# S5 outputs of a channel block as one group of eight matmuls, phase tables in a shared buffer

## The chip, the cores and the metric

The kernel runs on one core of a Trainium2 chip. The metric is the device time of one execution in microseconds; three executions of the kernel before took 1635.12, 1636.76 and 1636.93 us, so the median is 1636.76 us. A separate execution was recorded by the hardware profiler, and all traces and durations below are from that one.

## What is computed

One layer of a hybrid encoder on 256 tokens of width 2048, in float32. After a norm, `w_in` projects every token to 12288 columns. These feed three mixers (a gated linear recurrence called RG-LRU, a chunked attention, an S5 state space), and a sigmoid gate for each. The gated mixers are summed and projected by `w_out`; a SwiGLU feed-forward layer and a last norm follow. The change is in the S5 branch, which in the reference is

```python
bu_re = jnp.einsum("bsgh,gph->bsgp", ug, bb_re)      # 16 channels of group g -> 64 states
bu_im = jnp.einsum("bsgh,gph->bsgp", ug, bb_im)
_, _, xs_re, xs_im = lax.associative_scan(_complex_lin_op, (ar, ai, bu_re, bu_im), axis=1)
y = (jnp.einsum("bsgp,ghp->bsgh", xs_re, c_re) - jnp.einsum("bsgp,ghp->bsgh", xs_im, c_im))
y = y.reshape(b_, s_, SSM_W) + d * uf                # 1024 channels: 64 groups of 16
```

## The kernel before

**The main stream.** All large products run on TensorE as one long list of steps. A step loads 512 KB of weights (256 rows by 512 columns, the tile `raw`, three buffers, issued on the SP queue, L170), splits them into two parts of lower precision whose sum is exact (ScalarE casts `hi` at L123, VectorE subtracts to get `lo` at L124, seven buffers each), and multiplies them with the tokens: for both halves of the tokens and each of two weight tiles three matmuls, L198, L199 and L200, into the PSUM tiles `mm`. So a step has twelve matmuls of 512 columns, and PE has no pause between steps as long as `hi` and `lo` are there in time.

**Background work.** The three mixers are Python generators (`gen_lru`, `gen_att`, `gen_s5`). After each step `bg_mix` runs a few pieces of them, up to a budget; each `yield` states what the piece cost, and a negative number ends the generator's turn. This sets the order in which the program is written. A scheduler then orders the instructions of each engine: it may move an instruction ahead of ones written earlier where its operands and buffers allow it, and the weight loads and splits have a raised priority. Each engine then works through its own list, and semaphores hold an instruction until its operands are there.

**S5.** `gen_s5` treats the 1024 channels as eight blocks of 128 (`b`). A block has four state tiles of 128 states, `jj` 0 to 3, worked through in two halves of two tiles each (`sb`). For a block PE transposes the small B and C matrices and the input (L669 to L671), ScalarE copies `ct` (the C matrices, 32 channels for each state tile) and `uf` (the input) out of PSUM, `bu` and `bc` become operands for the input products. For each half:

- the phase tables: ScalarE scales a ramp (`q`, L702), VectorE reduces it (L703, L704; `w` is a second buffer), ScalarE takes the absolute value (L705), a sine (L706, `tab1`) and a cosine (L707, `tab0`);
- PE makes the input products `bu_re` and `bu_im` (L711, L712), and VectorE rotates them (L720 to L726), scans (L729, L730) and rotates back (L732 to L738), in `m1` and `m2` (tile `sA`) and `m3` and `m4` (tile `sB`). `m1` ends as the real part of the states (L734), `m2` as the imaginary part (L738);
- the output, `out_part`: for each of the two state tiles two matmuls (L745 for the real part, L746 for the imaginary) with a stationary operand of 128 x 32, so each uses one of four groups of 32 array columns and writes 32 PSUM partitions of `y_ps`. L748 adds the input times `d` for the 64 channels of the half and writes the result back to `u`.

The output of the first half is kept in a list (`pend`) until the tables of the second half have been written, that of the second half follows at the end of the block. `sA` has one buffer for `bu` and both halves, and so has `sB`; `q` and `w` have buffers of their own, `sq` and `sw`. All PSUM tiles of the mixers share four buffers (`sm`).

`drain("s5")` writes whatever is left of S5 when the main stream comes to the products that need its output, behind 224 steps; the GELU at L759 and two splits follow.

## Time and profile before

| | us |
|---|---|
| median of three executions | 1636.76 |
| the profiled execution, from its first to its last instruction | 1637.8 |
| PE busy with matmuls in it | 1612.1 |
| DVE busy | 1111.4 |
| ACT busy | 951.6 |
| matmuls L745 and L746, busy | 18.0 and 15.6 |
| first and last of them, start | 116.2 and 705.2 |

PE, DVE and ACT are TensorE, VectorE and ScalarE, and PEld is TensorE's loading of the stationary operand. A row of the timeline has the start in us from the span's first instruction, the length, the engine, the line, what is written and read, and how many instructions the row merges. The recorded end of a matmul is modelled and overlaps the next one; what one costs is read from the starts. A float32 matmul of this kind is two records, so the 64 matmuls in the program are 128 records in the trace.

### The profile page before, as it was taken

The page shows a single profiled execution, that of the slowest core. Times are in us where ns is not written, and L with a number is a line of the kernel's source. Part 1 is how long each engine was busy: PE and PEld are TensorE (multiplying, and loading weights), DVE is VectorE, ACT ScalarE, POOL GpSimd, SP SyncE. Part 2 cuts the span into 40 slices and gives each one's busy share as a digit, 9 for nine tenths or more (in the row PEclk, how much of TensorE's full clock was granted, in tenths as well). Part 3 has the DMA queues.
Part 4 walks back from the last instruction along what each step waited for, and adds up shares of the span by engine and source line. Part 5 has one row for each costly group of instructions (what it writes and reads, how often), then busy time and mean ns, then how long its engine had stood idle before and what let it go on. Part 6 is the DMA issues. An engine that isn't in the chain of part 4 may idle for free.

```text
span 1637.8 us, 21032 instructions
## 1 busy us (share of the span) xinstructions
PE 1612.1 (98%) x7263; PEld 1307.1 (80%) x7263; DVE 1111.4 (68%) x1910; ACT 951.6 (58%) x1696; POOL 0.8 (0%) x6
## 2 busy tenths in 40 slices
PE   7999999999999999999999999999999999999997
PEld 4877877778888777778888888888888888888886
DVE  4869889879697978876666555555555555555654
ACT  4677677675768676665455554555444455455443
POOL 0000000000000000000000000000000000000000
PEclk9999999999999999999999999999999999999999
DMA  8665566655554646565666666666666666666564
GB/s 224 198 178 150 166 183 185 186 165 174 165 177 146 197 152 214 170 201 185 214 236 182 193 191 190 185 192 190 187 192 196 193 187 194 190 192 186 188 191 144
DMA packets 169933, 304.21 MB, mean 186 GB/s; under 512 B 22185, under 2 KB 26721, under 8 KB 169057
## 3 DMA queue, kind: packets, MB, share of 16 engines
q1 hardware_dynamic: 153104, 292.66, 59.5%
q10 hardware_dynamic: 16720, 10.20, 2.3%
q8 instruction: 57, 0.93, 0.2%
q14 instruction: 52, 0.42, 0.1%
HBM read 300.71 MB, written 2.11 MB: 185 GB/s over the span
## 4 chain that ended last, share of the span: by engine, by line
PE 86%; DVE 5%; ACT 3%; DMA 3%; issue 2%; ACTq 0%; DVEq 0%
PE mm L199 27%; PE mm L200 27%; PE mm L198 27%; DMA raw<-in_w_in 3%; DVE lo L124 2%; ACT hi L123 1%; PE y_ps L746 1%; PE mm L957 1%; PE at_ps L241 1%; PE mm L956 1%; PE mm L958 1%; PE y_ps L745 0%; ACT bc L691 0%; DVE xc L470 0%; ACT bc L692 0%
## 5 line engine op out<-in xcount | busy, mean ns | idle before, releaser
L124 DVE TENSOR_TENSOR lo<-raw,hi 128x512 fp32r<-128x512 f32 x1088 | 736.9, 688 | 441.6 <-ACT hi L123 438.9
L123 ACT CAST hi<-raw 128x512 fp32r<-128x512 f32 x1088 | 658.7, 621 | 611.9 <-DVE lo L124 322.2
L199 PE MATMUL mm<-lo,xth 128*128 128x512 f32 x768 | 304.8, 397 | 2.6 <-DVE lo L124 2.6
L200 PE MATMUL mm<-hi,xtl 128*128 128x512 f32 x768 | 302.7, 394 | 0.0
L198 PE MATMUL mm<-hi,xth 128*128 128x512 f32 x768 | 284.2, 396 | 9.6 <-ACT hi L123 9.6
L200 PE MATMUL mm<-hi,h2l 128*128 128x512 f32 x704 | 275.0, 391 | 0.0
L198 PE MATMUL mm<-hi,h2h 128*128 128x512 f32 x704 | 274.9, 390 | 0.0
L199 PE MATMUL mm<-lo,h2h 128*128 128x512 f32 x704 | 274.0, 389 | 0.0
L198 PEld LDWEIGHTS mm<-hi,xth 128*128 128x128 f32 x768 | 144.0, 189 | 46.5 <-ACT hi L123 13.7
L199 PEld LDWEIGHTS mm<-lo,xth 128*128 128x128 f32 x768 | 145.0, 189 | 39.5 <-DVE lo L124 8.3
L200 PEld LDWEIGHTS mm<-hi,xtl 128*128 128x128 f32 x768 | 145.2, 189 | 29.4 <-issue 0.4
L199 PEld LDWEIGHTS mm<-lo,h2h 128*128 128x128 f32 x704 | 132.2, 188 | 27.3
L200 PEld LDWEIGHTS mm<-hi,h2l 128*128 128x128 f32 x704 | 132.1, 188 | 27.2
L198 PEld LDWEIGHTS mm<-hi,h2h 128*128 128x128 f32 x704 | 132.2, 188 | 26.8
L198 PE MATMUL mm<-hi,at 128*128 128x512 f32 x312 | 121.6, 390 | 0.0
L200 PE MATMUL mm<-hi,at 128*128 128x512 f32 x312 | 121.6, 390 | 0.0
L199 PE MATMUL mm<-lo,at 128*128 128x512 f32 x312 | 121.4, 389 | 0.0
L199 PEld LDWEIGHTS mm<-lo,at 128*128 128x128 f32 x312 | 58.6, 188 | 12.2
L200 PEld LDWEIGHTS mm<-hi,at 128*128 128x128 f32 x312 | 58.6, 188 | 12.2
L198 PEld LDWEIGHTS mm<-hi,at 128*128 128x128 f32 x312 | 58.6, 188 | 11.9
L200 PE MATMUL mm<-hi,mtl 128*128 128x512 f32 x128 | 50.3, 393 | 0.0
L199 PE MATMUL mm<-lo,yc 128*128 128x512 f32 x128 | 50.1, 391 | 0.0
(312 smaller groups left out, 1624.7 us busy)
## 6 DMA issues: line engine op xcount, KB each, us to landing
raw<-in_w_in SPq DMA_DIRECT2D x190, 512.0 KB, 4.2
raw<-in_w_ffn_gate SPq DMA_DIRECT2D x88, 512.0 KB, 4.0
raw<-in_w_ffn_up SPq DMA_DIRECT2D x88, 512.0 KB, 3.7
raw<-in_w_ffn_down SPq DMA_DIRECT2D x88, 512.0 KB, 4.7
raw<-in_w_branch SPq DMA_DIRECT2D x48, 512.0 KB, 4.1
raw<-in_w_out SPq DMA_DIRECT2D x32, 512.0 KB, 4.6
raw<-in_ssm_w_glu SPq DMA_DIRECT2D x16, 512.0 KB, 4.7
xa<-in_x SPq DMA_DIRECT2D x8, 256.0 KB, 3.8
```

The costliest lines, as they stand in the source:

```text
L123: act.copy(dst_hi, src)
L124: vec.tensor_sub(dst_lo, src, dst_hi.bitcast(F32))
L198: pe.matmul(acc[h], xh[:, k, hs], hi, start=k == 0, stop=False)
L199: pe.matmul(acc[h], xh[:, k, hs], lo, start=False, stop=False)
L200: pe.matmul(acc[h], xl[:, k, hs], hi, start=False, stop=k == kt - 1)
L241: pe.transpose(t[:, i * S + h * P:i * S + (h + 1) * P], src(h, kt0 + i), ident)
L746: pe.matmul(yp[rs, :S], ct[:, 1, rs], m2[:, i, :], start=False, stop=True)
L956: pe.matmul(last_acc[h], ah[:, k, hs], hi, start=k == 0, stop=False)
L957: pe.matmul(last_acc[h], ah[:, k, hs], lo, start=False, stop=False)
L958: pe.matmul(last_acc[h], al[:, k, hs], hi, start=False, stop=k == kt - 1)
```

## The change

```diff
-            bu = mx.tile([P, 2, 2, S], F32R, tag="sA", name="bu")
+            bu = mx.tile([P, 2, 2, S], F32R, tag="sA", name="bu", bufs=2)
...
+            ys = []
             for sb in range(2):
                 j0 = 4 * b + 2 * sb
-                q = mx.tile([P, 2, S], F32, tag="sq", name="sq")
-                w = mx.tile([P, 2, S], F32, tag="sw", name="sw")
+                qw = mx.tile([P, 2, 2, S], F32, tag="sB", name="qw")
+                q, w = qw[:, 0], qw[:, 1]
...
-                if pend:
-                    pend.pop()()
-                    yield 0.3
-                ma, mb = (mx.tile([P, 2, 2, S], F32, tag=t, name=t) for t in ("sA", "sB"))
+                ma = mx.tile([P, 2, 2, S], F32, tag="sA", name="sA", bufs=2)
+                mb = mx.tile([P, 2, 2, S], F32, tag="sB", name="sB")
...
-                def out_part(b=b, sb=sb, m1=m1, m2=m2, ct=ct, uf=uf, yb=yb):
-                    yp = sm("y_ps")
-                    for i in range(2):
-                        jj = 2 * sb + i
-                        rs = slice(32 * jj, 32 * jj + 32)
-                        pe.matmul(yp[rs, :S], ct[:, 0, rs], m1[:, i, :], start=True, stop=False)
-                        pe.matmul(yp[rs, :S], ct[:, 1, rs], m2[:, i, :], start=False, stop=True)
-                    rr = slice(64 * sb, 64 * sb + 64)
-                    vec.scalar_tensor_tensor(yb[rr], uf[rr], prm[rr, R_D + b:R_D + b + 1], yp[rr, :S],
-                                             ALU.mult, ALU.add)
-                pend.append(out_part)
+                ys.append((m1, m2))
                 yield 1.8
-                if sb == 1:
-                    yield -0.1
-                    pend.pop()()
-                    yield 0.3
+            yield -0.1
+            yp = sm("y_ps")
+            for part in range(2):
+                for jj in range(4):
+                    rs = slice(32 * jj, 32 * jj + 32)
+                    pe.matmul(yp[rs, :S], ct[:, part, rs], ys[jj // 2][part][:, jj % 2, :],
+                              start=part == 0, stop=part == 1)
+            vec.scalar_tensor_tensor(yb, uf, prm[:, R_D + b:R_D + b + 1], yp[:, :S], ALU.mult, ALU.add)
+            yield 0.3
```

The eight output matmuls of a block are now written together: the real parts of all four state tiles, then the imaginary parts. One `y_ps` takes all 128 channels, and one VectorE instruction (L748) finishes them. `sA` has a second buffer, so that the states of both halves live until then. `q` and `w` become two halves of a tile `qw` that takes turns with `m3` and `m4` in the one buffer `sB`. Line numbers shift a little: the tables stay at L702 to L707, the eight matmuls are all at L746, L748 is still the last step, and the rotations and scans between are two lower (the last addition of a half is L736 and was L738, the first products with the tables are L718 to L721 and were L720 to L723).

The list of PE around the output of the second block, first half, before:

```order
L198 MATMUL mm<-hi,xth 128x512
L746 MATMUL y_ps<-sA,ct 32x256
L745 MATMUL y_ps<-sA,ct 32x256
L746 MATMUL y_ps<-sA,ct 32x256
L199 MATMUL mm<-lo,xth 128x512
L200 MATMUL mm<-hi,xtl 128x512
```

and the middle of the second block's output now:

```order
L198 MATMUL mm<-hi,ya_1276 128x512
L199 MATMUL mm<-lo,ya_1276 128x512
L200 MATMUL mm<-hi,ya_1277 128x512
L746 MATMUL y_ps<-sA,ct 32x256 x4
L198 MATMUL mm<-hi,ya_1276 128x512
L199 MATMUL mm<-lo,ya_1276 128x512
```

The scheduler did not leave the matmuls where they were written. Before, a half's output stood in one piece of four matmuls (3 times of 16) or as a single real-part matmul and, some rows later, the other three (13 times): 29 visits of PE to this kind of work. Now it is one piece of eight (blocks 0 and 3) or, for the other six blocks, three pieces: the two real parts of the first half as soon as these are there, four matmuls (the real parts of the second half and the imaginary parts of the first, which use four different column groups), and the last two. That makes 20 visits.

The list of ACT around the tables of the second half of block 1, before (the tables made here are `tab_2458` and `tab_2457`; the `sq` and `sw` written behind them are already those of the next phase):

```order
L706 ACT_TABLE_LOAD
L706 ACTIVATE tab_2458<-sq 128x512
L702 ACTIVATE sq<-cst,s5par 128x256 x2
L123 CAST hi<-raw 128x512 x2
L346 ACT_TABLE_LOAD
L346 ACTIVATE merged<-merged 128x512
L707 ACT_TABLE_LOAD
L707 ACTIVATE tab_2457<-sw,cst 128x512
L123 CAST hi<-raw 128x512 x4
L705 ACTIVATE sw<-sq 128x512
```

and now, where all five belong to the same tables:

```order
L702 ACTIVATE qw<-cst,s5par 128x256 x2
L123 CAST hi<-raw 128x512
L519 DMA rbs<-in_attn_rel_bias 8x257
L123 CAST hi<-raw 128x512 x2
L705 ACTIVATE qw<-qw 128x512
L706 ACT_TABLE_LOAD
L706 ACTIVATE tab_2430<-qw 128x512
L123 CAST hi<-raw 128x512
L707 ACTIVATE tab_2429<-qw,cst 128x512
```

The ramp, the reduction and the absolute value no longer run a phase ahead, since their buffer is free only when the half before is done. The whole list of ACT has 35 loads of function tables, and had 32.

The list of DVE at the same place now, from the last addition of the first half (L736) to the first products of the second (L720, L718):

```order
L736 TENSOR_TENSOR sA<-sA,sB 128x512
L124 TENSOR_TENSOR lo<-raw,hi 128x512 x2
L663 TENSOR_TENSOR bx<-s5bb,cst 128x128 x2
L703 TENSOR_SCALAR qw<-qw 128x512
L124 TENSOR_TENSOR lo<-raw,hi 128x512
L704 SCALAR_TENSOR_TENSOR qw<-qw 128x512
L124 TENSOR_TENSOR lo<-raw,hi 128x512
L520 COPY rbs<-rbs 8x127
L124 TENSOR_TENSOR lo<-raw,hi 128x512
L720 TENSOR_TENSOR sA<-tab_2430,bu_im 128x512
L124 TENSOR_TENSOR lo<-raw,hi 128x512
L718 TENSOR_TENSOR sA<-tab_2429,bu_re 128x512
```

Before, L703 and L704 between two halves belonged to the tables of the next phase, and those of this one were already made. Between L704 and L718 stand three `lo` splits here, and two or three in the other blocks. In five of the eight blocks (this one among them) ACT also loads a function table ahead of L706 between the two halves.

More of the change, by code (lines that the diff above doesn't have):

```diff
@@ L650, in gen_s5 @@
         yield 1.8
-        pend = []
         for b in range(8):
```

## The prediction

> **What bounds the kernel now.** I read the page first: the busy time of each engine and the chain of work that ended last.
>
> ```profile
> span 1637.8 us, 21032 instructions
> PE 1612.1 (98%) x7263; PEld 1307.1 (80%) x7263; DVE 1111.4 (68%) x1910; ACT 951.6 (58%) x1696; POOL 0.8 (0%) x6
> PE 86%; DVE 5%; ACT 3%; DMA 3%; issue 2%; ACTq 0%; DVEq 0%
> ```
>
> PE is busy nearly all the time and carries 86% of the chain. So whatever PE no longer has to do comes off the end, as long as its operands keep up. S5's outputs run from 116 to 705 us, so I then read the busy times of that stretch beside those of the rest, and the groups and waits of the stretch.
>
> ```profile
> 100.00:707.00 607.00, 601.80 (x2748) 476.64 (x2747) 517.08 (x899) 420.12 (x789) 0.00 (x0) 1.00 0.59 175
> 707.00:1637.00 930.00, 921.68 (x4136) 762.00 (x4135) 531.09 (x812) 468.11 (x782) 0.00 (x0) 1.00 0.63 191
> PE mm L198 <- ACT hi L123: 3.1, 7, 0.9
> PE mm L199 <- DVE lo L124: 1.5, 3, 0.9
> L124 DVE TENSOR_TENSOR lo<-raw,hi 128x512 fp32r<-128x512 f32 x392 | 258.8, 684 | 67.5 <-ACT hi L123 66.3
> ```
>
> The columns of the first two rows are the stretch, its length, then the busy time of PE, PEld, DVE, ACT and POOL, the granted clock, the DMA share and GB/s. In the S5 stretch PE is idle for 607.0 - 601.8 = 5.2 us, of which 4.6 are waits for a `hi` or a `lo`. The clock is full. DVE is the next engine, with 517.1 of 607 us; it has 89.9 us idle, 66.3 of them waiting for a cast. DMA is no limit: without S5 the same kind of stream draws 191 GB/s, in the stretch only 175, and 12 us less would ask for 175 x 607 / 595 = 179.
>
> **What an output visit costs PE now.** The timeline of PE over the first block's first half shows both common shapes.
>
> ```profile
> 114.71 0.39 PE L198 MATMUL mm<-hi,xth 128*128 128x512 f32 x1
> ...
> 115.84 0.39 PE L200 MATMUL mm<-hi,xtl 128*128 128x512 f32 x1
> 116.16 0.62 PE L745 MATMUL y_ps<-sA,ct 128*32 128x256 f32 x2
> 116.71 0.50 PE L198 MATMUL mm<-hi,xth 128*128 128x512 f32 x1
> 117.05 0.39 PE L199 MATMUL mm<-lo,xth 128*128 128x512 f32 x1
> 117.28 0.40 PE L200 MATMUL mm<-hi,xtl 128*128 128x512 f32 x1
> 117.60 0.40 PE L746 MATMUL y_ps<-sA,ct 128*32 128x256 f32 x1
> 117.61 0.40 PE L745 MATMUL y_ps<-sA,ct 128*32 128x256 f32 x1
> 117.84 0.38 PE L746 MATMUL y_ps<-sA,ct 128*32 128x256 f32 x1
> 117.85 0.38 PE L745 MATMUL y_ps<-sA,ct 128*32 128x256 f32 x1
> 118.06 0.59 PE L746 MATMUL y_ps<-sA,ct 128*32 128x256 f32 x2
> 118.59 0.50 PE L198 MATMUL mm<-hi,xth 128*128 128x512 f32 x1
> 118.93 0.40 PE L199 MATMUL mm<-lo,xth 128*128 128x512 f32 x1
> ```
>
> A step of the main stream is (115.84 - 114.71) / 5 = 0.226 us, from start to start. The visit with one output matmul (two records) takes 117.05 - 115.84 = 1.21 us from the `mm` ahead to the second `mm` behind; two steps of the stream are 0.45, so the visit costs 0.76 us. The visit with three takes 118.93 - 117.28 = 1.65, so 1.20. Inside it L746 of one state tile and L745 of the next start 0.01 us apart and run beside each other: they use different groups of 32 array columns. The third matmul needs the group of the second and follows. So three matmuls are two rounds, a round costs 1.20 - 0.76 = 0.44 us, and the visit itself 0.76 - 0.44 = 0.32 us (0.32 us from the `mm` ahead in place of 0.23, and 0.5 in place of 0.39 for the first `mm` behind). The three visits with all four matmuls look like this:
>
> ```profile
> 209.91 0.39 PE L200 MATMUL mm<-hi,xtl 128*128 128x512 f32 x1
> 210.23 0.63 PE L745 MATMUL y_ps<-sA,ct 128*32 128x256 f32 x4
> 210.69 0.61 PE L746 MATMUL y_ps<-sA,ct 128*32 128x256 f32 x4
> 211.23 0.50 PE L198 MATMUL mm<-hi,xth 128*128 128x512 f32 x1
> 211.57 0.40 PE L199 MATMUL mm<-lo,xth 128*128 128x512 f32 x1
> ```
>
> From 209.91 to 211.57 is 1.66, less 0.45 is 1.21: two rounds, the L745 of both tiles beside each other and then both L746. In all, before: 13 visits of one (9.9 us), 13 of three (15.6) and 3 of four (3.6), together 29.1 us; of the shares, 29 x 0.32 = 9.3 us is for entering and leaving and 45 rounds make 19.8.
>
> **The same after.** The matmuls are the same 64 and none is shorter; what changes is how many run beside each other and how often PE goes there. By the instruction list there are 20 visits: 12 with two matmuls of one kind (two column groups, one round), 6 with four matmuls in four different column groups, and 2 with eight (all four groups twice). No row of the trace has more than two groups at once. Bounds: all four run beside each other, at 0.01 us for each further start, so a piece of four is one round and a piece of eight two; or only pairs do, so they are two and four rounds. The nearest row, the pair at 117.60, shows no slowing of either (0.44 us for the round, as for a lone matmul), so I take four at once, and 0.04 for the starts.
>
> - Four at once: 12 x 0.77 + 6 x 0.80 + 2 x 1.24 = 9.2 + 4.8 + 2.5 = 16.5 us. Saved: 29.1 - 16.5 = 12.6 us.
> - Pairs: 9.2 + 6 x 1.22 + 2 x (0.32 + 4 x 0.44) = 9.2 + 7.3 + 4.2 = 20.7 us. Saved: 8.4 us.
>
> The Trainium skill, "TensorE: Matmul & The Clock Gate", section on the measured speedup of packing small matmuls, has three column tiles at 2.38 times a single one, so 79% of full. By that, as an estimate, a round of four groups would be 0.44 / 0.79 = 0.56 us, ten such rounds (6 x 1 and 2 x 2) 1.2 us more than above, and the saving 11.4 us; the pair of this trace shows no such loss. The same part says that matmuls start and end strictly in order; the trace doesn't agree at 210.23, where the list has L745, L746, L745, L746 and both L745 ran first. The written order within a piece is therefore worth nothing by itself here.
>
> **The shared table buffer.** The engines' rows in the stretch:
>
> ```profile
> L738 DVE TENSOR_TENSOR sA<-sA,sB 128x512 f32<-128x512 f32 x16 | 10.9, 683 | 0.0
> L720 DVE TENSOR_TENSOR sA<-tab,bu_re 128x512 f32<-128x512 f32 x15 | 10.1, 677 | 0.1
> L704 DVE SCALAR_TENSOR_TENSOR sq<-sw,sq 128x512 f32<-128x512 f32 x14 | 9.6, 684 | 0.0
> L703 DVE TENSOR_SCALAR sw<-sq 128x512 f32<-128x512 f32 x14 | 5.9, 420 | 3.1 <-ACT tab L707 3.0
> L748 DVE SCALAR_TENSOR_TENSOR u<-uf,prm,y_ps 64x256 f32<-64x256 f32 x16 | 7.6, 476 | 0.7 <-PE y_ps L746 0.4
> L707 ACT ACTIVATE tab<-sw,cst 128x512 f32<-128x512 f32 x15 | 10.8, 717 | 0.0
> L706 ACT ACT_TABLE_LOAD x8 | 10.3, 1283 | 0.1
> L706 ACT ACTIVATE tab<-sq 128x512 f32<-128x512 f32 x15 | 9.5, 633 | 7.3 <-DVE sA L736 7.3
> L705 ACT ACTIVATE sw<-sq 128x512 f32<-128x512 f32 x14 | 8.8, 628 | 1.8 <-DVE sq L704 1.8
> ```
>
> Before, ramp, reduction and absolute value ran a phase ahead, and only sine and cosine waited for the old tables (7.3 us of ACT in all). Now L702 waits for the last addition of the half before (L738 in the row), 15 times, with the `hi` casts queued behind it on ACT; and DVE, with the `lo` splits behind it, cannot go past the first product with a new table until ACT has done L705 and L706: 0.628 + 0.633 = 1.26 us after L704, and L707 0.72 later. Between two blocks the operand work of the next block lies there. Between the halves of a block two or three `lo` of 0.684 do, so 1.37 us covers the 1.26. In five of the eight blocks a load of 1.283 comes ahead of L706: there DVE stands 1.26 + 1.28 - 1.37 = 1.2 us, together 6 us. If that cover were gone, it would be up to 2.5 us each time.
>
> Of these 6 us only what arrives at PE counts. The splits run ahead by up to seven buffers, and 89.9 us of idle DVE now leave PE 5.2 us of idle. Bounds: all 6 us arrive, or the new order also removes some of the present idle, at most 4.6 us. I take 1.5 us lost, nearer to nothing because of that ratio. Off the path: three more function table loads (3 x 1.28 = 3.8 us of ACT, in 187 us of its idle), eight instructions L748 in place of sixteen (8 x 0.476 = 3.8 us less DVE; the row's 256 elements in a row stay, only the partitions double). No load or DMA is added; those of `cr` on ACT's queue move by a few casts. The `y_ps` bank is held longer where the pieces lie apart: about 110 matmuls in block 1, 25 us, of four banks; the list has been made with that bank taken, so it changes the order and adds no work.
>
> **Sum.** -12.6 + 1.5 = -11.1 us. On the profiled execution 1637.8 becomes 1626.7. That execution is 1.0 us above the median of the timed ones, so the median 1636.76 becomes 1625.7 us. The last output now stands 38 `mm` matmuls earlier in the list (2597 of them ahead of it, before 2635), so GELU and its splits come earlier, not later.
>
> **The rivals.**
>
> - *Only two column groups run at once.* Saving 8.4, less 1.5: 1636.76 - 6.9 = 1629.9 us. For it: no row shows more than two. Against it: the pair costs no more than one, so nothing shared is visibly full. 0.12.
> - *DVE becomes the bound where S5 is dense, and the gain is waited away.* The freed 12.6 us come back as PE's waits for `lo`; then it is 1634 to 1638. For it: DVE is at 85% in the stretch, and the longest PE wait now is 0.9 us, so the lead has run out already. Against it: 66.3 of its 89.9 idle us are waits for casts that run ahead of PE. 0.11.
> - *The table chain now stands in front of the splits: slower.* If at each of the 15 turns DVE stood the whole 0.628 + 0.633 + 0.717 = 1.98 us behind L704, since the `lo` put there wait for casts queued behind L702, and PE with it, that is 29.7 us: 1636.76 - 12.6 + 29.7 = 1653.9 us. It decides from 12.6 / 15 = 0.84 us a turn. For it: ACT waited for DVE 7.3 us there already. Against it: those waits left PE almost nothing, and the `lo` between the halves belong to earlier casts. 0.06.
> - *The scheduler takes the group apart, so the change doesn't do what it says.* It does in six blocks of eight; that is in the sum already, through 20 visits in place of 8.
>
> **How the numbers follow.** The forecast has 0.71; its own range is 1621.5 (12.6 saved and most of today's 4.6 us of waits gone too, less a little) to 1630 (all 6 us arrive at PE). The pairs reach to 1634 at their worst, and I stop at 1631.5: that leaves out the absorbed gain and the slower case, and a little of the pairs. A measurement of this kernel can tell about 0.2%, or 3.3 us, from no change. Faster by more: forecast and pairs, 0.83. The absorbed gain is the same: 0.11. Slower: 0.06.
>
> **What would show it.** In the changed trace a piece of four `y_ps` matmuls starts within 0.04 us and is over, by starts, 0.80 us dearer than the stream; 1.2 would be pairs. Busy PE in the stretch falls, the stream's step stays 0.226. DVE's first product with a new table (L720) waits for ACT L706, about 1.2 us in five blocks; more, with PE rows waiting for `lo` adding up to over 10 us, would be the second or third rival. I am wrong at the root if PE's idle time in the stretch grows by as much as the visits shrink.

## The result, and the profile after

The changed kernel took 1654.99 us (median of four executions, 1653.72 to 1659.3); the kernel before, on the same chip, 1635.94 us. The ratio is 1.0117, 95% interval 1.0100 to 1.0133. So the change makes the kernel 19 us slower. The forecast was 1625.7 us. The profiled execution has a span of 1653.4 us (before 1637.8). These spans are 15.6 us apart and the medians 19: before and after were profiled in one execution each, and what is read from a trace below holds for that execution.

The page after, first its summary rows, then the chain of work that ended last:

```profile
span 1653.4 us, 21042 instructions
PE 1610.2 (97%) x7263; PEld 1303.0 (79%) x7263; DVE 1105.2 (67%) x1902; ACT 952.4 (58%) x1699; POOL 0.8 (0%) x6
PE 62%; DVE 17%; ACT 10%; DMA 6%; issue 4%; ACTq 0%; SPq 0%; DVEq 0%
```

PE is busy 1.9 us less, and its share of the chain has gone from 86% to 62%; DVE, ACT and DMA have taken it over. The two stretches, with the columns as before (length, busy PE, PEld, DVE, ACT, POOL, clock, DMA share, GB/s):

```profile
100.00:707.00 607.00, 584.41 (x2684) 460.45 (x2683) 501.57 (x875) 414.23 (x781) 0.00 (x0) 1.00 0.55 171
707.00:1637.00 930.00, 928.47 (x4161) 767.36 (x4160) 536.27 (x818) 472.99 (x789) 0.00 (x0) 1.00 0.61 193
```

In the S5 stretch PE now stands still for 607.0 - 584.4 = 22.6 us, where it was 5.2. The clock is full in both. DVE and ACT are *less* busy there than before (517.1 and 420.1), so no engine's work has grown; the work has moved in time. Counted from the trace, the main stream's matmuls number 192 to 2640 take 652.3 us, before 636.9: 15.4 us, nearly all of the 15.6 by which the spans differ (the start is 2.8 shorter and the end 3.1 longer).

The waits of PE, DVE and ACT in the S5 part that the argument uses (total, times, longest), after:

```profile
ACT hi L123 <- DMA raw<-in_w_in: 113.3, 83, 3.8
ACT hi L123 <- PE mm L200: 11.9, 10, 3.1
PE mm L198 <- ACT hi L123: 9.0, 9, 1.9
DVE sA L720 <- ACT tab L706: 6.5, 7, 1.5
PE mm L199 <- DVE lo L124: 6.3, 9, 2.3
ACT qw L702 <- DVE sA L736: 5.2, 4, 1.9
ACT qw L705 <- DVE qw L704: 3.4, 6, 0.9
PE bu_re L711 <- ACT bc L691: 2.8, 2, 1.7
```

PE's waits for `hi` and `lo` were 3.1 and 1.5 us and are 9.0 and 6.3; those at `bu_re`, for the operand copies `bc`, are new. The first two rows are ACT's own: its casts wait for weight loads (107.9 us before), and for PE to free one of the seven `hi` buffers, that is, with all of them full (28.5 us before, 11.9 now).

**The visits themselves came out as forecast.** PE's timeline at the middle of a block's output, and at a whole block in one piece:

```profile
282.39 0.39 PE L199 MATMUL mm<-lo,ya 128*128 128x512 f32 x1
282.62 0.40 PE L200 MATMUL mm<-hi,ya 128*128 128x512 f32 x1
282.95 0.64 PE L746 MATMUL y_ps<-sA,ct 128*32 128x256 f32 x8
283.52 0.50 PE L198 MATMUL mm<-hi,ya 128*128 128x512 f32 x1
283.85 0.39 PE L199 MATMUL mm<-lo,ya 128*128 128x512 f32 x1
...
210.93 0.40 PE L200 MATMUL mm<-hi,xtl 128*128 128x512 f32 x1
211.26 1.07 PE L746 MATMUL y_ps<-sA,ct 128*32 128x256 f32 x16
212.26 0.50 PE L198 MATMUL mm<-hi,xth 128*128 128x512 f32 x1
212.59 0.40 PE L199 MATMUL mm<-lo,xth 128*128 128x512 f32 x1
```

Four matmuls (eight records) in four different column groups: 283.85 - 282.62 = 1.23, less two steps of 0.226 is 0.78 us, against 0.76 for a single matmul before. Five of the six pieces of four cost this; the sixth, at 487.5 us, cost 1.21, with 0.4 us of it waiting for its states. Eight matmuls: 212.59 - 210.93 = 1.66, so 1.21. The 20 visits, up to the first `mm` behind each, are together 14.3 us; the 29 before were 25.5. With the 0.11 us that the second `mm` behind each visit is late, the saving is (25.5 + 3.2) - (14.3 + 2.2) = 12.2 us, and 12.6 was forecast. So 12 us of PE time went, and 15.4 + 12.2, some 27 us, of standing came in the stretch, counted from the starts of the matmuls. The idle time in the busy rows grew by less, 17.4 us: a main matmul is recorded as about 0.39 us long and the next one starts after 0.226, so the first 0.16 us of each pause do not show there.

### The profile page after: what moved, and what is told of

It reads as the page before. It is cut to its first block, busy times and chain, and to the rows that moved or that the text cites. A ratio compares the mean times of both kernels' runs of the same rounds, so it can differ in the third digit from the quotient of the medians.

```text
span 1653.4 us, 21042 instructions
## 1 busy us (share of the span) xinstructions
PE 1610.2 (97%) x7263; PEld 1303.0 (79%) x7263; DVE 1105.2 (67%) x1902; ACT 952.4 (58%) x1699; POOL 0.8 (0%) x6
## 4 chain that ended last, share of the span: by engine, by line
PE 62%; DVE 17%; ACT 10%; DMA 6%; issue 4%; ACTq 0%; SPq 0%; DVEq 0%
PE mm L199 20%; PE mm L200 20%; PE mm L198 20%; DVE lo L124 6%; DMA raw<-in_w_in 4%; ACT hi L123 2%; ACT bc L690 1%; DMA raw<-in_w_ffn_down 1%; ACT bc L691 1%; DVE sB L728 1%; ACT bc L688 1%; DVE sA L727 1%; PE at_ps L241 1%; DVE sB L721 1%; DVE sA L718 1%
## 5 line engine op out<-in xcount | busy, mean ns | idle before, releaser
L198 PE MATMUL mm<-hi,xth 128*128 128x512 f32 x768 | 286.5, 397 | 13.2 <-ACT hi L123 12.8
L199 PEld LDWEIGHTS mm<-lo,at 128*128 128x128 f32 x312 | 58.6, 188 | 12.2
```

Of the source, the lines that this page charges most:

```text
L198: pe.matmul(acc[h], xh[:, k, hs], hi, start=k == 0, stop=False)
L199: pe.matmul(acc[h], xh[:, k, hs], lo, start=False, stop=False)
```

## Where PE stands now

PE's loss is not spread over the stretch. At the start of each S5 block, from 6 us ahead of the block's operand copies to 6 us behind them, the same main matmuls fall back against before by 0.8, 3.4, 4.6, -1.0, -0.2, 2.7, 4.0 and 1.9 us: 16.2 of the 15.4 us, and the rest of the stretch comes out even. The time between one main matmul and the next, where no other work of PE can lie, shows the same: it grew by 15.0 us at the block starts and by 1.9 in the rest. This is the start of the seventh block, with 4.0. The timeline of ACT, after:

```profile
570.51 0.64 ACT L705 ACTIVATE qw<-qw 128x512 f32<-128x512 f32 x1
571.16 1.28 ACT L706 ACT_TABLE_LOAD   x1
572.46 0.63 ACT L706 ACTIVATE tab<-qw 128x512 f32<-128x512 f32 x1
573.10 1.65 ACT L690 CAST bc<-bu 32x256 fp32r<-32x256 f32 x4
574.78 0.62 ACT L123 CAST hi<-raw 128x512 fp32r<-128x512 f32 x1
...
575.83 0.73 ACT L707 ACTIVATE tab<-qw,cst 128x512 f32<-128x512 f32 x1
576.58 1.64 ACT L690 CAST bc<-bu 32x256 fp32r<-32x256 f32 x4
578.25 1.14 ACT L123 CAST hi<-raw 128x512 fp32r<-128x512 f32 x2
579.29 0.62 ACT L688 CAST bc<-bu 32x512 fp32r<-32x512 f32 x1
...
583.06 0.62 ACT L123 CAST hi<-raw 128x512 fp32r<-128x512 f32 x1
```

The timeline of DVE there (in brackets the idle time before the row and what ended it):

```profile
575.43 0.69 DVE L124 TENSOR_TENSOR lo<-raw,hi 128x512 fp32r<-128x512 f32 x1 [4.30 <-ACT hi L123]
583.71 0.69 DVE L124 TENSOR_TENSOR lo<-raw,hi 128x512 fp32r<-128x512 f32 x1 [3.52 <-ACT hi L123]
```

And that of PE:

```profile
578.92 0.73 PE L198 MATMUL mm<-hi,xth 128*128 128x512 f32 x2 [1.29 <-ACT hi L123]
583.73 0.74 PE L198 MATMUL mm<-hi,xth 128*128 128x512 f32 x2 [1.53 <-ACT hi L123]
```

At the start of a block ACT makes the twenty `bc` copies, four of 32 x 512 and sixteen of 32 x 256. They are short, but each is an instruction of 0.62 or 0.40 us: 4 x 0.62 + 16 x 0.40 = 8.9 us a block. ACT is busy without a pause for 11 to 16 us there and puts only 2 to 5 casts between them. PE takes a cast every six matmuls, 6 x 0.226 = 1.36 us, so 8 to 12 in that time. The difference is paid from the lead, the casts that are finished and not yet used. Counted from the trace, before the change the lead was 4.5 to 6 casts when the copies began and 0 to 1.5 when they ended: just enough, with 5.2 us of PE idle in the whole stretch. After it, the table work (L705, the load, L706 and L707, together 3.3 us) lies directly ahead of the copies or among them in this block and the third. The lead at the start of the copies is 1.5 casts here and 1.0 there, the two places with the largest losses; it is 2.5 at the second block (3.4 us lost) and 3.5 to 5.5 elsewhere. PE runs dry in the middle of the copies, and what it waits for, as DVE does, is a cast.

The place of the tables is not all that keeps the lead low. Between 554 and 564 us, ahead of the copies above, ACT stands still for 2.98, 1.17 and 3.16 us until a weight load has landed. So much of its idle time is no spare time in which it could make casts. No run here gives the loads more buffers, so whether they hold the lead down is open.

The reading makes two claims: that the copies take the saved time back, and that the shared buffer, through the place of the tables, makes it worse. The experiments test them, though most of them also get another list from the scheduler.

## The experiments

No kernel leaves out any computation, except the three with short copies. Times are medians; each group's kernel before ran on the same chip. "Idle" is PE's idle time in the stretch from 100 to 707 us, from the busy times by stretch; "stretch" the time of the main matmuls 192 to 2640 and "next 96" that of the 96 behind, where S5's output must be ready, both counted from the trace; "visits" the output visits up to the first `mm` behind. These four come from one profiled execution each. It can lie off the median: that of the fours 2.9 us below, that of the kernel before with six split buffers 8.0 above.

| kernel | us | ratio to before, 95% | visits | idle | stretch | next 96 |
|---|---|---|---|---|---|---|
| before | 1636-1641 | 1 | 25.5 | 5.2 | 636.9 | 21.8 |
| the change | 1654.99 | 1.0100-1.0133 | 14.3 | 22.6 | 652.3 | 21.8 |
| before, shared table buffer alone | 1661.35 | 1.0114-1.0150 | | 11.8 | 645.6 | 34.2 |
| before, one `yield` less | 1647.35 | 1.0030-1.0062 | | 6.4 | 646.4 | 21.8 |
| the change, old `yield` | 1659.81 | 1.0102-1.0141 | | 24.3 | 652.0 | 26.2 |
| before, pairs inside a half | 1641.57 | 0.9996-1.0017 | 20.1 | 8.9 | 635.6 | 23.4 |
| before, joint last addition | 1652.32 | 1.0059-1.0089 | 17.3 | 13.2 | 641.9 | 30.2 |
| before, six split buffers | 1662.19 | 1.0115-1.0168 | | 20.2 | 664.4 | 21.8 |
| the change, six split buffers | 1654.32 | 1.0069-1.0103 | | 16.8 | 651.9 | 21.8 |
| the change, own table buffers, six | 1641.86 | 1.0001-1.0020 | 15.9 | 12.7 | 640.8 | 21.8 |
| the same, list of the one above it | 1653.79 | 1.0076-1.0103 | | 16.8 | 652.0 | 21.8 |
| pairs, list held | 1636.43 | 0.9976-0.9996 | 19.9 | 6.7 | 633.4 | 21.8 |
| fours, list held | 1636.71 | 0.9973-0.9991 | 18.2 | 6.6 | 631.4 | 21.8 |
| before, short copies | 1629.56 | 0.9925-0.9962 | 22.4 | 1.2 | 626.5 | 21.8 |
| the change, short copies | 1629.33 | 0.9918-0.9947 | 16.0 | 5.0 | 624.9 | 21.8 |
| own table buffers, six, short copies | 1620.80 | 0.9867-0.9897 | 17.2 | 0.2 | 617.8 | 21.8 |
| before, copies on POOL | 1672.25 | 1.0188-1.0222 | | 7.5 | 629.3 | 60.1 |
| the change, copies on POOL | 1649.75 | 1.0051-1.0081 | | 9.5 | 624.0 | 45.2 |
| own table buffers, six, copies on POOL | 1633.77 | 0.9949-0.9975 | 15.7 | 7.5 | 625.5 | 28.4 |
| own table buffers, six, copies on both | 1624.40 | 0.9882-0.9915 | 16.2 | 3.3 | 622.7 | 21.8 |

### The parts of the change, one at a time

The shared buffer alone, in the kernel before:

```diff
-                q = mx.tile([P, 2, S], F32, tag="sq", name="sq")
-                w = mx.tile([P, 2, S], F32, tag="sw", name="sw")
+                qw = mx.tile([P, 2, 2, S], F32, tag="sB", name="qw")
+                q, w = qw[:, 0], qw[:, 1]
```

> The kernel before with one edit: the ramp and its reduction (q, w) live in the buffer of m3 and m4, as in the change; outputs, yields and the single buffer of the states are as before. PE's visits to the output stay 29, so nothing is saved. Theory A (the shared buffer makes ACT wait at L702 and puts the whole table chain among the copies of the next block's operands): slower than before by what the change lost beside its saved visits, 12 + 17 to 19 = about 29 us, at least 15; PE's waits for hi, lo and bc rise from 7 us to over 20. Theory B (the pace: a yield of 0.3 per block is gone, and background work bunches earlier): within 3 us of before. Theory C (any new order costs some us): slower by 3 to 10.

Measured: 21.6 us slower, more than the whole change. 8.7 us of it lie in the stretch. The other 12.4 are behind it: S5's last output comes so late that the first products with `yc` wait. The waits of PE in this kernel, as before:

```profile
PE mm L198 <- ACT yc L123: 7.5, 1, 7.5
PE mm L199 <- DVE lo L124: 7.1, 8, 2.0
```

The theory that the shared buffer costs (A, at least 15 us) holds for the total, but it had no place for the loss at the end. The change has the same buffer and no such wait at the end, so it doesn't add up from parts.

The change also drops one `yield 0.3` per block, a number by which the planner counts what it has written. The kernel before without it, and the change with it put back ahead of the second half's rotations:

```diff
                 if pend:
                     pend.pop()()
-                    yield 0.3
```

```diff
                 yield -1.4
+                if sb == 1:
+                    yield 0.3
                 ma = mx.tile([P, 2, 2, S], F32, tag="sA", name="sA", bufs=2)
```

> The kernel before with one edit: the yield of 0.3 behind the delayed output of the first half is left out, as it is in the change; nothing else. The background then runs ahead by up to some 40 main matmuls at the end, as in the change. Theory A (shared buffer): within 3 us of before. Theory B (pace): slower by 15 us or more. Theory C (any new order costs some us): slower by 3 to 10.

> The whole change with one edit: the yield of 0.3 is put back, at the place where the first half's output stood, so that the background keeps the pace of the kernel before. Theory A (shared buffer): stays slower than before, 1645 to 1660 us. Theory B (pace): the saved visits show, 1622 to 1630 us. Theory C: anywhere between 1630 and 1650.

Measured: without it the kernel before, with identical instructions, is 7.6 us slower; the change with it is no better than the change (ratios 1.0121 and 1.0117). The first is what theory C forecast, the second what theory A did. So the order of the lists alone can be worth 8 us, but the lost `yield` doesn't explain the change. What in the new order costs the 7.6 us wasn't settled: idle of PE over 100 to 707 is only 1.2 us more.

### Fewer, fuller visits without the buffers

The kernel before with the two real parts of a half ahead of the two imaginary parts (the first), and with the last additions of a half's real and imaginary states joined in one instruction, so that all four matmuls of a half become ready together (the second):

```diff
-                    for i in range(2):
-                        jj = 2 * sb + i
-                        rs = slice(32 * jj, 32 * jj + 32)
-                        pe.matmul(yp[rs, :S], ct[:, 0, rs], m1[:, i, :], start=True, stop=False)
-                        pe.matmul(yp[rs, :S], ct[:, 1, rs], m2[:, i, :], start=False, stop=True)
+                    for part, m in enumerate((m1, m2)):
+                        for i in range(2):
+                            jj = 2 * sb + i
+                            rs = slice(32 * jj, 32 * jj + 32)
+                            pe.matmul(yp[rs, :S], ct[:, part, rs], m[:, i, :], start=part == 0, stop=part == 1)
```

```diff
-                vec.tensor_mul(m3, sn, m4)
-                vec.tensor_sub(m1, m1, m3)
-                yield 1.8
+                vec.scalar_tensor_tensor(m3, sn, -1.0, m4, ALU.mult, ALU.mult)
...
+                yield 1.8
...
-                vec.tensor_add(m2, m2, m4)
+                vec.tensor_add(ma, ma, mb)
```

> The kernel before with one edit: within a half's output the two real-part matmuls come ahead of the two imaginary ones, so that each pair uses two column groups. No buffer and no yield is touched. By the terms of the prediction, 13 visits of one (0.76) and 13 of three (1.20) become 26 of two (0.77 each): 13 x (1.96 - 1.54) = 5.5 us saved, the three visits of four unchanged. Theory A and B: 1629 to 1633 us. Theory C (any new order costs some us): up to 1640.

> The kernel before with the two real-part matmuls of a half ahead of the two imaginary ones, and with the last subtraction and addition of a half made one addition of 1024 elements (the sign goes into the product before it), so that real and imaginary part are ready at the same time and the scheduler leaves the four matmuls of a half in one piece. No buffer is touched. Visits: 16 x 1.21 = 19.4 us in place of 29.1, so 9.7 us saved on PE. Theory A: 1627 to 1633 us on the scale of 1638. Theory D (saved PE time is waited away): within 3 us of before. The last output stands at 2672 main matmuls, close to the 2688 at which its result is needed, so up to 5 us can be lost there.

Measured: the visits fall by 5.4 and 8.2 us, where 5.5 and 9.7 were costed. The first kernel is no faster; the second is 12 us slower, of which 8.4 are again a late last output. In neither did the saved PE time arrive in the time, and both forecasts (1629 to 1633 and 1627 to 1633 us) failed.

### The same edit with every list held

Were the visits' savings lost, or was it the new lists? Two kernels have the edit of the pairs above, but PE, ACT, DVE and SP work through the order of the kernel before (constraints on the order of issue alone, with no wait added). In the first only the two middle matmuls of each half change places; in the second all four stand together, at the place of the later ones, in 8 of 13 halves.

> The same edit as in the run with the parts inside a half (real parts of both state tiles first), but with the lists of PE, ACT, DVE and SP held to those of the kernel before: every instruction of ACT, DVE and SP in the same order, and on PE only the output matmuls exchanged, two in the place of the first and two in the place of the other three. Theory D (PE time saved in the stretch is waited away, whatever the list): within 2 us of before. Theory F (the visits' price is right and arrives; what went wrong in the other runs is that every edit made the scheduler write another list, with other stalls): the 13 x (1.96 - 1.54) = 5.5 us arrive, 0.3% faster than before.

> As the run before, and in eight of the thirteen halves all four output matmuls stand at the later place, so that a visit is left out; the rest of all lists is again that of the kernel before. Visits: 11 x 1.21 + 10 x 0.77 = 21.0 us in place of 29.1, so 8.1 us less PE. Theory D: within 2 us of before. Theory F: 7 to 8 us, 0.45 to 0.5% faster than before.

Measured: 0.14% and 0.18% faster, and the stretch is 3.5 and 5.5 us shorter for 5.6 and 7.3 us less in visits. So with the lists held 63 and 75% of the saving arrive in the stretch of the profiled execution, but in the medians only 2.6 and 2.3 us, less than half. The second was profiled in an execution 2.9 us under its median, so the medians are the safer figure. Neither theory had this: the one said less than 2 us, the other 5.5 and 7 to 8. Both kernels beat the kernel before, by little. The copies are the same twenty here, so where the lists stay they don't take everything back.

### The shared buffer and the buffers that it saves

Own table buffers need room: with seven split buffers they don't fit in SBUF beside the second `sA`. So all three have six `hi` and `lo` (`HBUF = 6` in place of 7): the kernel before, the change, and, with the second edit as well, the change with `sq` and `sw` of their own:

```diff
-HBUF = 7
+HBUF = 6
...
-                qw = mx.tile([P, 2, 2, S], F32, tag="sB", name="qw")
-                q, w = qw[:, 0], qw[:, 1]
+                q = mx.tile([P, 2, S], F32, tag="sq", name="sq")
+                w = mx.tile([P, 2, S], F32, tag="sw", name="sw")
```

> The kernel before with six buffers of hi and lo in place of seven, to be the base for the next two (that is the room which two more table buffers need). Both theories: somewhat slower than before, 1 to 10 us, since the splits run less far ahead.

> The change with six buffers of hi and lo. Both theories: 15 to 25 us slower than the kernel before with six buffers, as with seven.

> The change with six buffers of hi and lo, and ramp and reduction back in buffers of their own: the group of eight matmuls without the shared table buffer. Theory A (the shared buffer is what costs): at least 15 us faster than the change with six buffers, and no slower than the kernel before with six; if all of the saved visits arrives, 12 us faster than that. Theory D (the group itself costs: PE's list meets the products and operands of the background earlier than ACT and DVE have them, so that PE time saved in the visits is waited away): within 5 us of the kernel before with six buffers, with PE's waits for hi, lo and bc higher by 8 to 12 us. Theory E (the sharing costs little where the outputs are grouped): within 5 us of the change with six buffers.

Measured: with six buffers the change is 12.5 us slower with the shared buffer than without (1654.32, 1641.86). Six split buffers cost the kernel before 22 us and the change nothing (1.0086 against 1.0117), so the depth of the splits and the order of the lists can't be taken apart as a plain sum. All three expectations failed: the kernel before was to lose 1 to 10 us, the change with six was to be 15 to 25 us slower than it and is 7.9 faster, and own table buffers fit none of the theories A, D and E. Which kernel is the base matters: own table buffers and six split buffers are 1.4 us slower than the kernel before with seven, and 20.3 us faster than the kernel before with six. In the first comparison the time between one main matmul and the next grows by 9.4 us at the block starts and by 0.2 in the rest. The lead there is 3.5 to 5 casts when the copies begin and falls to 0 in seven of eight blocks; how much of that the missing seventh buffer makes, no run shows. Between the two changed kernels with six buffers that time differs by 8.8 us at the block starts and by 3.3 in the rest.

Is it the wait for the buffer or the order? A kernel with own table buffers, but with its lists held to those of the change with six buffers:

> The change with six buffers of hi and lo and with own buffers for ramp and reduction, but all lists held to those which the scheduler wrote for the change with six buffers and the shared table buffer: the waits for the shared buffer are gone, the order that it forced is kept. Theory A (the waits themselves cost): near the same kernel with its own list, 0 to 3 us above before. Theory G (the order costs: tables written late, among the operand copies of the next block, whatever they wait for): near the change with six buffers, 12 to 15 us above before.

Measured: 1653.79 us, as slow as the shared buffer itself (1.0089 against 1.0086). Its waits:

```profile
PE mm L198 <- ACT hi L123: 10.0, 11, 3.1
DVE sA L720 <- ACT tab L706: 8.6, 6, 2.5
PE mm L199 <- DVE lo L124: 4.4, 8, 1.0
```

No wait at L702 for the buffer is left, and nothing has come back, as theory G said. So here it is the order that costs, tables made late, right where they are needed, and not the wait for the buffer.

### The copies shortened

The test of the other claim: the twenty copies of a block become four, of 96 partitions each. These kernels leave out the placing of the matrices and the input, so the S5 output means nothing; all other work is there.

```diff
-                for k in range(3):
-                    d = slice(32 * k, 32 * k + 32)
-                    if k == 0:
-                        act.copy(bc[d, jj], buf[r, 0])
-                    else:
-                        act.copy(bc[d, jj, 0], buf[r, k // 2, 0])
-                        act.copy(bc[d, jj, 1], buf[r, k % 2, 1])
+                act.copy(bc[:96, jj], buf[:96, 0])
```

> The kernel before, with the twenty operand copies of a block into bc (L688 to L691 of before) replaced by four copies of 96 partitions, one for each state tile. The rows of the matrices and the input are then no longer put in their places, so the S5 output means nothing; every other instruction is there, with the same sizes. A copy of 32 x 512 takes 0.62 us and one of 32 x 256 0.40, so a block's copies fall from 11 to 16 us with the casts between them to about 2.5 us. Theory ACT-burst (the lead of the casts is used up by these copies, and PE's saved time is lost there): PE's stalls between 100 and 725 fall from 6.7 us to 2 to 4 us, since the operand copies cost the list of before little: 1633 to 1638 us. Theory list (any rewritten list costs 5 to 15 us): 1642 to 1655 us.

> The changed kernel with the same four copies in place of twenty (its S5 output means nothing either). Theory ACT-burst: stalls fall from 27 us to under 10, and the grouped output's saved time arrives: 8 to 12 us under the run of before with short copies, 1624 to 1630 us. Theory table buffer (the tables late in each half, whatever the copies do): the stalls stay over 18 us and the time 10 us or more above the run of before with short copies. Theory list: anything between, with no relation to the copies.

> The changed kernel with separate table buffers and six split buffers, and the four copies in place of twenty. With the twenty copies the own buffers were worth 12.5 us (1641.9 against 1654.3). Theory ACT-burst: the shared buffer costs mainly because its tables come to lie beside the copies, so with four copies the two changed kernels are within 4 us of each other. Theory table buffer: own buffers are still worth 8 us or more.

Measured: the busy times of the stretch, before with short copies, the change, and the change with its own table buffers, in this order:

```profile
100.00:707.00 607.00, 605.79 (x2795) 485.49 (x2794) 520.46 (x902) 383.15 (x683) 0.00 (x0) 1.00 0.59 177
```

```profile
100.00:707.00 607.00, 602.05 (x2801) 482.98 (x2800) 517.67 (x898) 376.04 (x686) 0.00 (x0) 1.00 0.60 178
```

```profile
100.00:707.00 607.00, 606.76 (x2834) 489.94 (x2833) 522.33 (x902) 385.70 (x691) 0.00 (x0) 1.00 0.60 180
```

PE's idle time falls to 1.2, 5.0 and 0.2 us. Short copies alone make the kernel before 10.7 us faster, more than either theory said (3 of it because its list has cheaper visits now, 22.4). With own table buffers and six split buffers the grouped output is then worth another 8.8 us (1620.80 against 1629.56), where with twenty copies the same kernel gained nothing on before. Of the 8.8 the visits make 5.2 (22.4 against 17.2); most of the rest is that pauses between one main matmul and the next are 3.6 us shorter. The change itself goes from 19 us above the kernel before on its chip to 10.9 below, but is only level with the kernel before with short copies, not 8 to 12 us under it: the shared buffer still costs 8.5 us (1629.33 against 1620.80, seven split buffers against six), where it was 12.5 with twenty copies. So it takes the copies for the grouping's gain to be lost, as the first theory has it; but its expectation that with short copies the shared buffer is nearly free fails, while the rival's 8 us or more holds and its stalls of over 18 us do not. The buffer is a second cost, two thirds of which stay without the copies. The waits for the tables in the change with short copies are as large as in the change:

```profile
DVE sA L713 <- ACT tab L699: 8.1, 6, 2.1
ACT qw L698 <- DVE qw L697: 4.8, 6, 0.9
```

(L713, L699, L698 and L697 are L720, L706, L705 and L704 of the change.)

### The copies on another engine

The same with the whole computation: the twenty copies written for POOL, which does 0.8 us of work in the kernel.

```diff
-                        act.copy(bc[d, jj], buf[r, 0])
+                        nc.gpsimd.tensor_copy(bc[d, jj], buf[r, 0])
```

(and so for the other two lines)

> The kernel before with the twenty operand copies of a block written for GpSimd, which does next to nothing in the kernel (0.8 us), in place of ScalarE; the computation is whole. Theory copies (ScalarE's copies cost the list of before about 10 us, by the run with short copies): 1627 to 1634 us against 1639 to 1640 of before, if GpSimd's copies come in time. Rival (GpSimd's copies are slower than ScalarE's, some 1 us or more each, and PE then waits at the input products bu_re for bc, or they slow VectorE down): not faster than before, and the longest wait in the stretch is that of bu_re.

> The changed kernel with its own table buffers and six split buffers, with the same copies on GpSimd; the computation is whole. Theory copies: the grouped output arrives as it did with short copies (8.8 us of a possible 10), so 6 to 10 us under the run of before with copies on GpSimd, about 1620 to 1627 us, and a kernel that beats both. Rival (GpSimd too late or in VectorE's way): the two runs on GpSimd are within 4 us of each other, or slower than before.

> The changed kernel, shared table buffer and all, with the copies on GpSimd; the computation is whole. With short copies it was 8.5 us above the one with its own table buffers and equal to before with short copies. Theory copies and table buffer as two separate costs: 6 to 10 us above the run with own table buffers on GpSimd, and within 4 us of before on GpSimd. If the shared buffer cost only through ScalarE's copies: within 4 us of the one with its own buffers.

Measured: the stretch shrinks in all three, by 7.6 us (before), 28.3 (the change) and 15.3 (own table buffers). But all three pay at its end, the kernel before most. With the copies on POOL the eighth block of the kernel before begins its copies at 706 us, where it was 648, and S5's last output stands directly ahead of the products that need it. POOL's copies take longer on average, but that this is why the scheduler wrote such a list isn't shown. PE's longest waits in the kernel before and in the change, with the copies on POOL:

```profile
PE y_ps L745 <- DVE sA L734: 16.7, 2, 9.0
```

```profile
PE y_ps L746 <- DVE sA L732: 14.1, 1, 14.1
```

All three expectations failed by that, which neither theory had priced: the rival had the wait at `bu_re`, and it is at the outputs. The kernel with own table buffers, at 1633.8 us above its 1620 to 1627, still beats both kernels, by 0.38% against before. Here the shared buffer costs 16.0 us in all, where 6 to 10 were expected, but nothing in the stretch (624.0 and 625.5); it shows at its end (45.2 and 28.4). So how it costs differs from list to list.

The last run shares the copies out, four long ones on ACT and sixteen short ones on POOL, with own table buffers and six split buffers:

```diff
-                        act.copy(bc[d, jj, 0], buf[r, k // 2, 0])
-                        act.copy(bc[d, jj, 1], buf[r, k % 2, 1])
+                        nc.gpsimd.tensor_copy(bc[d, jj, 0], buf[r, k // 2, 0])
+                        nc.gpsimd.tensor_copy(bc[d, jj, 1], buf[r, k % 2, 1])
```

> The changed kernel with its own table buffers and six split buffers, and of the twenty copies of a block the four of 32 x 512 on ScalarE and the sixteen of 32 x 256 on GpSimd; the computation is whole. In the list S5's last output stands 124 matmuls ahead of the products that need it (13 with all copies on GpSimd). Theory copies (ScalarE's copies take the grouped output's gain, and with all of them on GpSimd it was S5 being late that cost): no wait at the end of S5, 2640 to 2736 at 21.8 us, the stretch at 620 to 626 us (636.9 before, 640.8 with all copies on ScalarE), and 1620 to 1629 us. Rival (copies on GpSimd slow the rest as such): the stretch stays at 630 us or more, or the time is no better than the 1633.8 of all copies on GpSimd.

Measured: 1624.40 against 1641.01 us, 0.9898 (0.9882 to 0.9915), 16.6 us faster than before and the best version with the whole computation. All of the first theory's numbers hold: 21.8 us behind the stretch, 622.7 us in it. The kernel before with its copies shared out in this way was not run, so how much of the 16.6 us is the grouping's and how much the copies' isn't known. The busy times of this kernel:

```profile
PE 1597.6 (99%) x7263; PEld 1303.0 (80%) x7263; DVE 1112.2 (69%) x1902; ACT 905.0 (56%) x1570; POOL 76.0 (5%) x134
```

All of PE's waits for operands of the main stream in the S5 part:

```profile
PE mm L198 <- ACT hi L123: 2.4, 2, 2.2
PE mm L199 <- DVE lo L124: 0.3, 1, 0.3
```

And its groups of copies on POOL (busy, mean ns, idle before):

```profile
L690 POOL CAST bc<-bu 32x256 fp32r<-32x256 f32 x64 | 40.8, 638 | 544.7 <-ACT bu L123 542.3
L691 POOL CAST bc<-bu 32x256 fp32r<-32x256 f32 x64 | 34.4, 538 | 3.3
```

## Why the prediction was wrong, point by point

Two steps failed. The saving of 12.6 us at PE was carried into the time in full, and the order that the shared buffer forces was priced at 1.5 us.

- *What bounds the kernel.* Read too coarsely. PE is busy 98%, but "whatever PE no longer has to do comes off the end, as long as its operands keep up" left the condition to averages: ACT has 187 us idle in the stretch, 121 of them waiting for weight loads, and none in the 11 to 16 us at each block's start. The runs with short copies and the last run point to ACT's copies there as what sets the pace: the same grouping is worth 8.8 us without them and nothing with them.
- *The visits, -12.6.* Right: 12.2 measured. A piece of four costs 0.78 (0.80 forecast), of eight 1.21 (1.24). The rival with only two groups at once is refuted. "Saved at PE" was not "saved in time", which is the step that failed first: with own table buffers the grouping brought nothing against before (ratio 1.0001 to 1.0020, with six split buffers in place of seven).
- *The shared table buffer, +1.5.* The wait itself is as worked out: 6 us of DVE behind the tables, 6.5 measured. The price was mis-sized, by five to eight times: 12.5 us with six buffers, and 8.5 with short copies. It was taken as a wait and discounted by the ratio 89.9 to 5.2. That ratio is an average over the whole stretch; where the lead is used up, idle of DVE can go through to PE. And the held list shows that the cost stays when the wait for the buffer is taken away. I had costed moved instructions only by their own time, and the ones moved past by nothing.
- *The three more table loads, off the path.* On average ACT's idle time has room for them; at 571.16 one stands right ahead of the copies.
- *The end of S5 comes earlier, not later.* Right here (21.8 us for the next 96 matmuls in both). Where it failed, in seven of the other kernels, it cost 1.6 to 38 us.
- *Rivals.* The slower one, that the table chain stands in front of the splits, gave 1653.9 us, and 1655.0 was measured. The tables' place does cost, but the number agrees by luck: DVE stood 6.9 us behind the tables, not 29.7. DVE as the bound is refuted: it is less busy, and its splits wait longer for casts than before. The right rival, ACT's copies as the limit at block starts, was missing. The group of the splits in the stretch, after (78.1 us of waits for casts, before 66.3):

```profile
L124 DVE TENSOR_TENSOR lo<-raw,hi 128x512 fp32r<-128x512 f32 x379 | 250.0, 681 | 78.6 <-ACT hi L123 78.1
```

- *"I am wrong at the root if PE's idle time in the stretch grows by as much as the visits shrink."* It grew by 17.4 us against 12.2, so by its own sign the prediction was wrong at the root.

What the runs account for: the 12 us saved at PE don't arrive (with own table buffers the time is 1.4 us up, not 12 down), and the shared buffer's order costs 12.5 more. That makes 14 us slower, the change with six split buffers. The change as given is 19 us slower than before. The two changed kernels themselves differ by only 0.7 us (1654.99 and 1654.32): the other 5 us lie in the kernel before, which took 1635.94 us on the one chip and 1640.44 on the other. It was not found why six split buffers hurt the kernel before and not the change. Most of these kernels have a list of their own, and a list alone was worth 8 us, about as much as either cost with short copies. So a share of the lists in both costs isn't excluded: they are likely in sign, since several runs agree, and known only to some us in size.

## What to carry to other kernels

Ask of the stage, not of the average, which engine's burst uses up the lead that feeds the bottleneck: count what the bottleneck takes in that time, what is made, and what is in stock. Time saved on the busiest engine arrives only where that lead lasts, so shorten or move the burst first; in these runs the saving then came. A buffer that two stages share is an order, not only a wait; price the instructions that come to stand behind each other, and look where the last of a side branch is due.

## What was not expected of the hardware

- Four matmuls of 128 x 32 in four column groups cost a visit 0.78 us, a single one 0.76. The Trainium skill, "TensorE: Matmul & The Clock Gate", section "Measured speedup vs the span model", has 2.38 times for three column tiles; this trace shows no loss even for four.
- A copy of 32 partitions cost ACT as much as one of 128: 0.62 us for 512 elements in a row, where the `hi` casts of 128 x 512 take 0.62 too, and 0.40 for 256. The Trainium skill, "ScalarE: Activation LUTs", section "What ACT_TABLE_LOAD costs", counts 186 ns and 0.833 ns for each element of a row, as an estimate 0.40 and 0.61; the trace agrees. It also has instructions behind each other overlap by 93 ns. The trace shows that for casts and for the 96-partition copies, and not for the 32-partition ones (the first timeline row from the change with own table buffers and short copies, the second from the last run):

```profile
534.52 2.19 ACT L684 CAST bc<-bu 96x512 fp32r<-96x512 f32 x4
```

```profile
549.01 2.51 ACT L688 CAST bc<-bu 32x512 fp32r<-32x512 f32 x4
```

  Four take 2.19 and 2.51 us: with 0.62 us for the last, 0.52 and 0.63 from start to start. Why wasn't tested.
- POOL needed 0.54 and 0.64 us on average for the 32 x 256 copies that ACT does in 0.40 (the rows of the last run; the shortest there took 0.39), and VectorE's splits were slower in the stretch with them, 0.702 us against 0.684 before. The group in the last run:

```profile
L124 DVE TENSOR_TENSOR lo<-raw,hi 128x512 fp32r<-128x512 f32 x398 | 270.9, 702 | 65.7 <-ACT hi L123 64.5
```

- Identical instructions in another order cost 7.6 us (0.46%), after one number of the planner was changed.
